# First K and V tiles of a linear attention kernel loaded as two transfers of 16 and 112 partitions

## The chip, the cores and the metric

One core of a Trainium2 chip runs the kernel. The metric is device time in microseconds (us). Before the change it is 126.86 us, the median of 3 runs (126.85 to 126.97).

## The reference

Linear attention with ReLU features, for 8 batches of 12 heads, 512 positions and 64 dimensions, in float32:

```python
Q_feat, K_feat = np.maximum(0, Q), np.maximum(0, K)
KV = np.einsum('bhkd,bhkv->bhdv', K_feat, V)          # 64 x 64 for each head
K_sum = np.sum(K_feat, axis=2)
numerator = np.einsum('bhqd,bhdv->bhqv', Q_feat, KV)
denominator = np.einsum('bhqd,bhd->bhq', Q_feat, K_sum)
return numerator / (denominator[..., None] + 1e-10)
```

Q, K, V and the output have 12.58 MB each, so 37.75 MB are read and 12.58 MB written.

## The kernel before

The 96 heads are worked in 12 octets of eight heads. An octet of K, V, Q or output is 1 MB of float32 that lies in one piece in memory; it is viewed as 128 partitions of 8 KB (`RQ * D` = 32 x 64 numbers), each partition being 32 positions of one head, so that 16 partitions make a head.

**Loads.** Octets 1 to 11 come through GpSimd's queue: `load_kv(g)` fetches K and V of four heads at a time (L99, L101), `load_q(o)` a whole Q octet (L105), all cast to bf16 on the way. They are issued in order in a loop at the top (L115 to L118); `kin` and `vin` have 12 buffers and `qin` 7. The K and V of octet 0 are the exception: they are loaded as float32, each by one transfer of 128 partitions, K from SyncE (SP, L111) and V from ScalarE (ACT, L112), into `k8` and `v8` (named `k_first` and `v_first` in the profile), two buffers of the pool that later holds the output tiles. The order of work is written out by hand; the tile framework adds only the waits that data needs.

**Octet 0.** `prep8` makes the bf16 operands: DVE writes `kf` (ReLU of K times a mask, L152) and half of `vo8` (V times a mask, L157), ACT the other half (L156). `qt(0)` transposes Q on TensorE (L208) and ACT applies the ReLU (L216). `mm_kv8` accumulates K^T V in PSUM over 32 matmuls (L163), and ACT copies the blocks out (L167).

**Octets 1 to 11.** `prep` and `prep_v` (L173, L175, L180, L182) make the operands of four heads, `mm_kv` (L187) the products, `evac_kv` (L197) the copies, `denom` (L258 to L270) the reciprocals of the denominators, `out_t` (L238, L240) the transposed numerators, `back` (L276) their transposes, and `norm` (L282) the product of the two on DVE.

**Stores.** `store(o)` issues one store of 1 MB from SP (L298), the last octet in two halves (L296). Ahead of each of the first seven stores SP issues a small transfer ("probe", L291) that reads 2 to 14 partitions of the K tile of five octets later, which holds the stores back until that tile has landed:

```python
    def store(o, o_sb):
        if o + DELAY < NO:
            n = PROBE[o]
            nc.sync.dma_start(out=scratch[0:n], in_=k_sb[2 * (o + DELAY)][0:n, 0, :])
```

Of the kernel before, what the change touches and what calls it, by code (L numbers as in the profile page):

```python
# [10 lines left out]
def kernel(  # L11
# [7 lines left out]
    nc = tc.nc  # L19
    B, H, S, D = Q.shape  # L20
    assert D == 64
    P = 128
# [35 lines left out]
    def view(X, f):  # L58
        return X.rearrange("b h s d -> (b h s d)").rearrange("(n p f) -> n p f", p=P, f=f)
# [43 lines left out]
    def load_q(o):  # L103
        q_sb[o] = qin.tile([P, U, 2 * D], bf16, name="q_sb")
        nc.gpsimd.dma_start(out=q_sb[o].rearrange("p u f -> p (u f)"), in_=Qr[o], single_packet=True)  # L105


    K8, V8 = view(K, RQ * D), view(V, RQ * D)
    k8 = outp.tile([P, RQ, D], fp32, name="k_first", tag="o_sb")
    v8 = outp.tile([P, RQ, D], fp32, name="v_first", tag="o_sb")  # L110
    nc.sync.dma_start(out=k8.rearrange("p r d -> p (r d)"), in_=K8[0])  # L111
    nc.scalar.dma_start(out=v8.rearrange("p r d -> p (r d)"), in_=V8[0])  # L112
    load_q(0)
    make_identity(nc, ident)
    for o in range(1, NO):  # L115
# [288 lines left out]
```

## Time and profile before

| | |
|---|---|
| median of 3 runs | 126.86 us |
| the profiled execution | 126.98 us |
| its span, first to last instruction | 125.2 us |
| busy share of the span: PE, DVE, ACT, POOL | 68%, 67%, 64%, 26% |
| HBM read and written over the span | 402 GB/s |
| DMA packets | 10349 |
| `k_first` and `v_first` issued | 0.74 us |
| first use of `k_first` (DVE L152) and `v_first` (ACT, before L156) | 9.55 and 9.81 us |
| first probe issued by SP | 43.19 us |

The profile is of one execution. Its busy shares are those of the compute engines; the DMA rows give the mean share of 16 DMA engines and the bytes that they moved (counted where they are written, so a load with a cast to bf16 counts half of what it reads). q0 is the queue of GpSimd's transfers, q1 that of SP's, q10 that of ACT's. "To landing" is the time from a transfer's issue until all of it has arrived. A stretch's DMA share can come out slightly over 1, since neighbouring packets of an engine overlap.

### The profile page before, as it was taken

The numbers are of one execution on the slowest core, as the hardware profiler recorded it, in microseconds if no ns is written. First come the engines' busy times: TensorE is split into PE (matmuls) and PEld (weight loads), VectorE is DVE, ScalarE is ACT, GpSimd is POOL, SyncE is SP. The second block draws the span as 40 slices with busy tenths as digits, with TensorE's granted clock in tenths as the row PEclk, the third lists the DMA queues.
The fourth block names the chain that finished last, engine by engine and source line by source line (L and its number), as shares of the span: only waits on it lengthen the run. The fifth ranks groups of instructions, "written<-read, shape, count | busy, mean of one in ns | idle before, by whom it ended". The sixth has DMA issues, their size and how long they took to land.

```text
span 125.2 us, 2684 instructions
## 1 busy us (share of the span) xinstructions
PE 85.7 (68%) x1075; PEld 77.4 (62%) x1075; DVE 83.5 (67%) x192; ACT 80.7 (64%) x112; POOL 32.1 (26%) x62
## 2 busy tenths in 40 slices
PE   0005795598988899895498499399777587797500
PEld 0005465497878789783597398299576486696400
DVE  2719715979799797979348746935928918979600
ACT  0008959969898998989159468666839646837100
POOL 6902624414344241142133124033122000000000
PEclk9999999999999999999679769959999999999995
DMA  2999999999999999999999999999999999999992
GB/s 84 390 325 205 217 205 209 219 202 217 205 214 210 209 215 320 263 213 290 294 212 276 310 211 249 334 213 216 349 232 217 330 254 212 321 423 424 424 412 116
DMA packets 10349, 32.68 MB, mean 261 GB/s; under 512 B 1249, under 2 KB 1249, under 8 KB 8673
## 3 DMA queue, kind: packets, MB, share of 16 engines
q0 software_dynamic: 8064, 17.83, 74.4%
q1 hardware_dynamic: 2128, 13.64, 26.8%
q10 hardware_dynamic: 144, 1.05, 2.1%
q8 instruction: 8, 0.13, 0.4%
q14 instruction: 5, 0.03, 0.1%
HBM read 37.75 MB, written 12.58 MB: 402 GB/s over the span
## 4 chain that ended last, share of the span: by engine, by line
DMA 33%; DVE 28%; PE 24%; ACT 5%; issue 3%; DVEq 1%; ACTq 0%; POOLq 0%
DMA v_sb<-in_V_dram 14%; DVE o_sb L282 13%; DMA q_sb<-in_Q_dram 13%; PE ps_kv L187 8%; DMA v_first<-in_V_dram 7%; PE ps_bk L276 6%; DVE kf L173 4%; PE ps_kv L163 4%; PE ps_qt L208 4%; DVE vo_all L175 3%; DVE vo_all L182 2%; ACT vo_all L156 2%; DVE den L266 2%; ACT qt L216 2%; DVE rec L270 1%
## 5 line engine op out<-in xcount | busy, mean ns | idle before, releaser
L282 DVE TENSOR_TENSOR o_sb<-ps_bk,rec 128x1024 f32<-128x1024 f32 x24 | 28.3, 1218 | 15.3 <-PE ps_bk L276 15.3
L187 PE MATMUL ps_kv<-vo_all,kf 128*128 128x132 bf16 x352 | 25.9, 232 | 6.6 <-DVE vo_all L182 6.1
L187 PEld LDWEIGHTS <-kf 128*128 128x128 bf16 x352 | 23.7, 104 | 7.9 <-issue 4.3
L208 PE MATMUL ps_qt<-ident,q_sb 128*128 128x128 bf16 x192 | 16.0, 250 | 16.7 <-DMA q_sb<-in_Q_dram 16.7
L216 ACT ACTIVATE qt<-ps_qt 128x1024 bf16<-128x1024 bf16 x23 | 22.4, 1024 | 6.3 <-PE ps_qt L208 6.2
L197 ACT CAST kvd<-ps_kv 64x260 bf16<-64x260 f32 (+1 forms) x46 | 16.6, 360 | 15.1 <-PE ps_kv L187 13.9
L208 PEld LDWEIGHTS <-q_sb 128*128 128x128 bf16 x192 | 14.2, 114 | 17.7 <-DMA q_sb<-in_Q_dram 17.6
L240 ACT COPY ot_sb<-ps_ot 128x1024 f32<-128x1024 f32 x22 | 22.0, 1014 | 1.9 <-PE ps_ot L238 1.0
L276 PE MATMUL ps_bk<-ident,ot_sb 128*128 128x128 f32 x192 | 23.0, 273 | 0.0
L173 DVE TENSOR_SCALAR kf<-k_sb,mask 128x1024 bf16<-128x1024 bf16 x44 | 18.3, 458 | 6.4 <-DMA k_sb<-in_K_dram 6.4
L99 POOL DMA_DIRECT2D k_sb<-in_K_dram x22 | 12.2, 555 | 37.1 <-DMA q_sb<-in_Q_dram 17.2
L276 PEld LDWEIGHTS ps_bk<-ident,ot_sb 128*128 128x128 f32 x192 | 20.8, 141 | 0.0
L101 POOL DMA_DIRECT2D v_sb<-in_V_dram x22 | 12.5, 566 | 18.3 <-DMA k_sb<-in_K_dram 10.2
L238 PE MATMUL ps_ot<-qt,kvd 128*128 128x256 bf16 x88 | 12.7, 271 | 4.3 <-DVE o_sb L282 4.3
L238 PEld LDWEIGHTS <-kvd 128*128 128x128 bf16 x88 | 8.2, 97 | 6.3 <-issue 5.7
L180 ACT ACTIVATE vo_all<-v_sb,mask 128x1024 bf16<-128x1024 bf16 x10 | 11.5, 1153 | 0.2
L175 DVE TENSOR_SCALAR vo_all<-v_sb,mask 128x1024 bf16<-128x1024 bf16 x22 | 10.7, 485 | 1.3 <-DMA v_sb<-in_V_dram 1.3
L258 PEld LDWEIGHTS <-qt 128*128 128x128 bf16 x192 | 6.7, 96 | 4.9 <-ACT qt L216 2.0
L258 PE MATMUL ps_den<-kvd,qt 128*128 128x16 bf16 x192 | 7.3, 179 | 3.0 <-ACT kvd L167 1.7
L105 POOL DMA_DIRECT2D q_sb<-in_Q_dram x12 | 7.0, 580 | 7.6 <-DMA v_sb<-in_V_dram 4.8
L156 ACT ACT_TABLE_LOAD x1 | 1.3, 1283 | 9.8 <-DMA v_first<-in_V_dram 9.8
L182 DVE TENSOR_SCALAR vo_all<-v_sb,mask 128x1024 bf16<-128x1024 bf16 x12 | 5.8, 484 | 0.0
(35 smaller groups left out, 48.3 us busy)
## 6 DMA issues: line engine op xcount, KB each, us to landing
out_dram<-o_sb SPq DMA_DIRECT2D x11, 1024.0 KB, 8.8
q_sb<-in_Q_dram POOLq DMA_DIRECT2D x12, 512.0 KB, 14.7
k_sb<-in_K_dram POOLq DMA_DIRECT2D x22, 256.0 KB, 14.1
v_sb<-in_V_dram POOLq DMA_DIRECT2D x22, 256.0 KB, 13.2
v_first<-in_V_dram ACTq DMA_DIRECT2D x1, 1024.0 KB, 9.0
k_first<-in_K_dram SPq DMA_DIRECT2D x1, 1024.0 KB
out_dram<-o_sb SPq DMA_DIRECT2D x2, 512.0 KB, 5.0
scratch<-k_sb SPq DMA_DIRECT2D x1, 1.0 KB
```

The costliest lines, as they stand in the source:

```text
L101: nc.gpsimd.dma_start(out=v_sb[g].rearrange("p r d -> p (r d)"), in_=Vr[g], single_packet=True)
L173: nc.vector.tensor_scalar(kf[g][:, :, s, :], k_sb[g], scalar1=0.0, scalar2=mask[:, 0, s:s + 1], op0=Alu.max, op1=Alu.mult)
L175: nc.vector.tensor_scalar(vo[g % NB][:, :, 0, 2:D + 2], v_sb[g], scalar1=mask[:, 1, 0:1], scalar2=None, op0=Alu.mult)
L187: nc.tensor.matmul(ps_kv[:, g % 2, 0:2 * (D + 2)].rearrange("p (t d) -> p t d", t=2), kf[g][:, r, :, :].rearrange("p s d -> p (s d)"), vo[ ...
L197: copy(kvd[o % NK][64 * c:64 * c + 64, 4 * gs.start + s:4 * gs.stop:2, c * D1:c * D1 + D1].rearrange("p (g t) d -> p g t d", t=2), ps_kv[6 ...
L208: nc.tensor.transpose(ps[:, u, :], q_sb[o][:, i * (U // 2) + u, :], ident)
L216: nc.scalar.activation(to, ps, Act.Relu)
L238: nc.tensor.matmul(ps[:, i], kvd[o % NK][:, h, 1:2 * D + 1], q[:, :, h, :], start=True, stop=True, skip_group_check=True)
L240: nc.scalar.copy(ot[o][:, :, 4 * j:4 * j + 4], ps.rearrange("p h u c -> p u h c"))
L258: nc.tensor.matmul(ps[:, u], qt_sb[o % NZ][:, u, :], kvd[o % NK][:, :, 0:2 * D1:2 * D1 - 1], start=True, stop=True, skip_group_check=True)
L276: nc.tensor.transpose(ps[:, 2 * v:2 * v + 2].rearrange("p c d -> p (c d)"), ot[o][:, 8 * j + v].rearrange("p h c -> p (h c)"), ident32)
L282: nc.vector.tensor_tensor(o_sb[:, rs], ps, rec[o][:, rs].unsqueeze(2).to_broadcast([P, 16, D]), op=Alu.mult)
```

## The change

The two loads of 128 partitions become four: partitions 0 to 15 of K (SP) and of V (ACT), and then partitions 16 to 127 of each, on the same two queues. The tiles, the bytes and all that follows are the same.

```diff
     k8 = outp.tile([P, RQ, D], fp32, name="k_first", tag="o_sb")
     v8 = outp.tile([P, RQ, D], fp32, name="v_first", tag="o_sb")
-    nc.sync.dma_start(out=k8.rearrange("p r d -> p (r d)"), in_=K8[0])
-    nc.scalar.dma_start(out=v8.rearrange("p r d -> p (r d)"), in_=V8[0])
+
+    for rows in (slice(0, 16), slice(16, P)):
+        nc.sync.dma_start(out=k8[rows].rearrange("p r d -> p (r d)"), in_=K8[0][rows])
+        nc.scalar.dma_start(out=v8[rows].rearrange("p r d -> p (r d)"), in_=V8[0][rows])
     load_q(0)
     make_identity(nc, ident)
```

## The prediction

> **What bounds the kernel now.** I read the page first (slices, queues, issues), then the busy time by stretch at both ends, then the chain of waits and the timeline of the first microseconds. The slices and the queues:
>
> ```profile
> span 125.2 us, 2684 instructions
> ...
> DMA  2999999999999999999999999999999999999992
> GB/s 84 390 325 205 217 205 209 219 202 217 205 214 210 209 215 320 263 213 290 294 212 276 310 211 249 334 213 216 349 232 217 330 254 212 321 423 424 424 412 116
> ...
> q1 hardware_dynamic: 2128, 13.64, 26.8%
> q10 hardware_dynamic: 144, 1.05, 2.1%
> ```
>
> From the second slice to the last but one the 16 DMA engines are at 9 of 10, while no compute engine passes 68% of the span. (The rates near 210 are loads that GpSimd issues with a cast to bf16, so the bytes written are half of those read; the engines are as full there.) Only the first slice (0 to 3.1 us) and the last have room. The two ends in the view of busy time by stretch (columns: stretch, its length, PE, PEld, DVE, ACT and POOL busy, clock, DMA share, GB/s):
>
> ```profile
> 1.50:2.00 0.50, 0.00 (x0) 0.00 (x0) 0.25 (x1) 0.00 (x0) 0.50 (x2) 1.00 0.40 66
> 2.00:2.50 0.50, 0.00 (x0) 0.00 (x0) 0.17 (x3) 0.00 (x0) 0.42 (x3) 1.00 0.46 131
> 2.50:3.00 0.50, 0.00 (x0) 0.00 (x0) 0.23 (x3) 0.00 (x0) 0.50 (x2) 1.00 0.85 262
> 3.00:3.50 0.50, 0.00 (x0) 0.00 (x0) 0.23 (x3) 0.00 (x0) 0.50 (x1) 1.00 0.81 344
> 3.50:4.00 0.50, 0.00 (x0) 0.00 (x0) 0.17 (x2) 0.00 (x0) 0.50 (x2) 1.00 1.02 426
> ...
> 115.00:120.00 5.00, 2.60 (x26) 2.30 (x23) 3.08 (x4) 1.16 (x2) 0.00 (x0) 1.00 1.00 422
> ```
>
> The engines take two microseconds to get from nothing to 426 GB/s, and only `k_first` and `v_first` feed them then. At 115 to 120 us they run at 422 GB/s on stores alone. Is that the end of a queue, or the pace of compute? The timeline and the issues answer:
>
> ```profile
> 0.74 0.41 ACTq L112 DMA_DIRECT2D v_first<-in_V_dram  x1
> 0.74 0.39 SPq L111 DMA_DIRECT2D k_first<-in_K_dram  x1
> 1.24 0.66 POOL L105 DMA_DIRECT2D q_sb<-in_Q_dram  x1 [0.79 <-POOLq L388]
> ```
>
> ```profile
> v_first<-in_V_dram ACTq DMA_DIRECT2D x1, 1024.0 KB, 9.0
> ...
> out_dram<-o_sb SPq DMA_DIRECT2D x2, 512.0 KB, 5.0
> ```
>
> A last half store moves 524 KB, 1.24 us at 422 GB/s, yet takes 5.0 us to land: about 3.8 us of stores stand before it. So compute has some 3.8 us to spare at the tail, and the kernel ends when the DMA engines have moved everything. The chain of waits agrees in the middle: it runs through compute until 47.5 us, then sits on `v_sb` landing (14% of the span) and `q_sb` landing (13%). A microsecond of DMA time lost or won at the start therefore reaches the end whole.
>
> **Part 1: issues and packets, priced at nothing on the path.** One more issue on SP (0.39 us, by the L111 row) and one on ACT (0.41 us, L112). SP's next instruction is the first probe at 43.2 us; ACT's is the table load before L156, which waits for V until 9.81 us. If that cover were gone they would cost 0.4 us each. GpSimd's Q load at 1.24 us is on a sequencer of its own and is not moved. The second K transfer is queued behind the first on SP and issues at about 1.13 to 1.52 us; the present one issued at 0.74 and its first bytes move after 1.5 us, so it should be there by some 2.3 us. Packets: in q10, 144 are 128 rows of 8 KB and 16 completions. In q1, 128 rows of K, 11 x 128 and 2 x 128 rows of stores, and the seven probes' 56 rows make 1848; 14 whole transfers give 224 completions, which leaves 56, one for each row of the probes. So a transfer of few rows goes one row to an engine, and one of 16 rows puts one 8 KB row on each of the 16. A row at full rate is 8192 B by 426/16 GB/s = 0.31 us. The 32 added completions are 2 small packets per engine, a few hundredths of a microsecond at most.
>
> **Part 2: the ramp, a gain.** Summing the stretches, by 4.0 us (0.5 x (66+131+262+344+426)) KB = 615 KB have moved, which is 1.44 us at 426 GB/s: the ramp is worth a start at 4.0 - 1.44 = 2.56 us. The first bytes move in the stretch from 1.5 us; if rows on all engines began at about 1.8, that would be 0.75 us better. If the ramp is the time in which a transfer's rows are handed out, a transfer of an eighth of the rows shortens it; if it is the latency of the first reads, it stays. Bounds 0 and -0.75, and nothing in the trace separates them; I take -0.3, nearer to nothing because the share of 0.40 to 0.46 with little moved says that engines already hold packets and wait on them.
>
> **Part 3: the 16-row slices, a loss.** K's rows 0 to 15 and V's rows 0 to 15 (262 KB) now stand at the head of both hardware queues on every engine, and the other rows are behind them. At 426 GB/s they take 0.62 us, as the same bytes do now. [...] Bounds: 0.62 us (nothing lost) and, at the 66 GB/s of the poorest stretch, 4.0 us (3.4 lost). I take the 131 GB/s of 2.0 to 2.5 us, the stretch nearest to this case: both queues under way, but not all engines delivering. 262 KB by 131 GB/s is 2.0 us, so +1.4. The rows behind do not fill the hole, since they are behind on the same queues, and Q's load has not arrived (GpSimd's transfers move only when the GB/s fall below 400, after 5 us).
>
> [...]
>
> **Part 4: the other 112 rows.** [...] Bounds: at 426 GB/s the remaining 1.84 MB take 4.3 us, nothing lost; at 344 GB/s, the poorest stretch with both queues full, 5.3 us, so +1.0. I take +0.4, below the middle since GpSimd's loads join from 5 us and fill what is left free.
>
> **Part 5: waits.** DVE's L152 and ACT's L156 wait for two completions instead of one. Behind L152 stands all of DVE, behind L156 the copies that PE's L163 needs. A wait by itself is 17 ns (the semaphore instructions at L298). K and V would land 1 to 2 us later than now (9.6 and 9.7 us), and the compute chain starts later by as much; that hides under the loads it waits for from 47.5 us on and the 3.8 us at the tail, and the loads themselves are late by the same amount.
>
> **Sum:** -0.3 + 1.4 + 0.4 + 0.0 = +1.5 us. The profiled execution took 126.98 us (span 125.2 and 1.8 around it), so 128.5 by it; the median of the runs is 0.12 lower, and so I forecast 128.4 us.
>
> **Rivals.**
>
> *The early start pays (faster).* The 16 rows go through at 426 GB/s and wake all engines at once; the second transfers arrive before the two rows per engine (0.62 us) are done. Price: part 2 at its -0.75 end or less, parts 3 and 4 at nothing: 126.1 to 126.5 us, middle 126.3. For it: the ramp is the only unfilled stretch before the tail, and every engine gets a row. It decides where the two slices take less than about 1.0 us together, since then part 3 costs less than the ramp gives. [...] Chance 0.28.
>
> *It moves nothing (same).* Either the slices' loss and the ramp's gain cancel (0.4 to 0.7 us each), or the ramp is read latency and the 16 rows flow freely, which leaves the completions: 126.7 to 127.0 us. For it: the same bytes move by the same engines. Chance 0.08.
>
> *The bad end of my own case.* The slices at 66 GB/s and the 112 rows at +1.0 would give +3.4 + 1.0 - 0.3 = +4.1, 131.0 us. Both ends together are unlikely; I count 0.07 for anything above 129.8, inside the chance of slower.
>
> **How the numbers follow.** Slower 0.64 (forecast, 127.2 to 129.8 its own range), same 0.08, faster 0.28; "same" is within 0.2%, 0.25 us, about what a measurement of this kernel can tell from no change. The range: 129.8 leaves 0.07 above; reaching down to 126.2 takes in most of the rival, with about 0.08 below. That is 126.2 to 129.8.
>
> **What would show it.** Right or wrong on part 1: q10 with 160 packets and q1 with 2144. Part 3: a stretch of about 2 us after 1.8 us with a high DMA share at 100 to 150 GB/s; the rival would show 400 GB/s before 3 us. Part 4: 340 to 426 GB/s afterwards, `v_first` landing past 10.5 us. The end: the first probe on SP, now at 43.2 us, and the last stores later by the same 1.5 us; stores at 422 GB/s to the last. I am wrong if K and V land before 9.5 us, or if they land late and the probes do not move.

## The result and the profile after

The change makes the kernel slower: 129.05 us (median of 4 runs, 128.95 to 129.19) against 126.91 us, a ratio of 1.0169 with a 95% interval of 1.0152 to 1.0187. The profiled execution took 129.19 us, its span is 127.4 us against 125.2.

The slices and queues of the changed kernel's page:

```profile
span 127.4 us, 2689 instructions
...
DMA  5999999999999999999999999999999999999993
GB/s 95 221 293 233 211 217 205 210 212 208 214 208 221 202 214 269 309 215 241 334 216 239 342 215 216 345 234 219 305 271 214 301 279 214 304 413 419 427 405 148
...
q1 hardware_dynamic: 2144, 13.64, 27.7%
q10 hardware_dynamic: 160, 1.05, 3.1%
```

The two queues have the 16 more packets each that 16 more completions make. The DMA engines are as full as before, and even fuller in the first slice (5 tenths against 2), but the second and third slices move 221 and 293 GB/s where they moved 390 and 325. From the fourth on the two rows look alike. So the engines are busy and deliver less, at the start only. Packets overlap a little: over the whole span the queues' shares add up to 104.4% of the 16 engines' time (103.8% before the change). The stretches of the start say when (columns as before: stretch, length, the five engines, clock, DMA share, GB/s). They count a packet, with all its time and its bytes, in the stretch in which it starts; that is how a share can be 1.57, well over 1:

```profile
1.50:2.00 0.50, 0.00 (x0) 0.00 (x0) 0.25 (x1) 0.00 (x0) 0.50 (x2) 1.00 0.87 197
2.00:2.50 0.50, 0.00 (x0) 0.00 (x0) 0.17 (x3) 0.00 (x0) 0.42 (x3) 1.00 1.40 246
2.50:3.00 0.50, 0.00 (x0) 0.00 (x0) 0.23 (x3) 0.00 (x0) 0.50 (x2) 1.00 0.77 98
3.00:3.50 0.50, 0.00 (x0) 0.00 (x0) 0.23 (x3) 0.00 (x0) 0.50 (x2) 1.00 1.57 164
3.50:4.00 0.50, 0.00 (x0) 0.00 (x0) 0.17 (x2) 0.00 (x0) 0.50 (x2) 1.00 0.66 82
4.00:5.00 1.00, 0.00 (x0) 0.00 (x0) 0.92 (x5) 0.00 (x0) 1.00 (x3) 1.00 0.83 213
5.00:6.00 1.00, 0.00 (x0) 0.00 (x0) 0.89 (x3) 0.00 (x0) 1.00 (x3) 1.00 1.01 295
6.00:8.00 2.00, 0.00 (x0) 0.00 (x0) 0.53 (x13) 0.00 (x0) 0.16 (x1) 1.00 0.97 281
```

Three phases can be read from it. To 2.5 us the changed kernel is ahead by the rows that have started: 0.5 x (197+246) = 222 KB against 98 KB, a lead of 123 KB or 0.29 us at 426 GB/s. From 2.5 to 5 us it moves 98, 164, 82 and 213 GB/s where the kernel before moved 262, 344, 426 and 410; by 5.0 us it has 607 KB against 1025, 0.98 us behind. From 5 to 8 us it runs at 281 to 295 GB/s, and there it loses the rest. The queues from 5 to 7 us (packets, MB, share of the 16 engines' time), before the change and then after it:

```profile
q1 hardware_dynamic: 37, 0.30, 37.1%
q10 hardware_dynamic: 37, 0.30, 36.0%
q0 software_dynamic: 31, 0.13, 31.4%
```

```profile
q10 hardware_dynamic: 37, 0.30, 52.1%
q1 hardware_dynamic: 33, 0.27, 46.0%
```

The same 37 rows of V took 36.0% of the engines' 2 us and now take 52.1%: 0.31 and 0.45 us a row (share x 2 us x 16 engines / 37). GpSimd's loads (q0) have no packet here after the change; their first ones come in the stretch from 7 to 8 us, two microseconds later than before. The loads behind them are late as well: the first probe on SP, whose time is set by a load of octet 5, is issued at 45.25 us, 2.06 later.

```profile
45.25 0.78 SPq L293 DMA_DIRECT2D scratch<-k_sb  x1
```

After that nothing is lost or won; the span ends 2.2 us later. K and V are first used at 12.3 and 12.4 us, 2.7 and 2.6 us later than before:

```profile
12.26 1.42 DVE L154 TENSOR_SCALAR kf<-k_first,mask8k 128x1024 bf16<-128x1024 f32 x2 [5.45 <-DMA k_first<-in_K_dram]
12.43 1.28 ACT L158 ACT_TABLE_LOAD   x1 [12.43 <-DMA v_first<-in_V_dram]
```

### The profile page after: what moved, and what is told of

The parts are those of the page before. It is cut to its first block, busy times and chain, and to the rows that moved or that the text cites. A ratio compares the mean times of both kernels' runs of the same rounds, so it can differ in the third digit from the quotient of the medians.

```text
span 127.4 us, 2689 instructions
## 1 busy us (share of the span) xinstructions
PE 88.0 (69%) x1075; PEld 78.8 (62%) x1075; DVE 83.4 (65%) x192; ACT 80.6 (63%) x112; POOL 31.4 (25%) x62
## 3 DMA queue, kind: packets, MB, share of 16 engines
q1 hardware_dynamic: 2144, 13.64, 27.7%
## 4 chain that ended last, share of the span: by engine, by line
DMA 77%; PE 8%; DVE 6%; issue 2%; POOL 2%; DVEq 1%; ACT 0%; POOLq 0%
DMA k_sb<-in_K_dram 31%; DMA q_sb<-in_Q_dram 25%; DMA v_sb<-in_V_dram 21%; DVE o_sb L284 4%; PE ps_bk L278 4%; PE ps_kv L189 2%; DVEq L401 1%; PE ps_qt L210 1%; DVE kf L175 1%; DVE qt L216 1%; PE ps_den L227 1%; POOL q_sb L105 0%; PE ps_ot L253 0%; DVE kvd L199 0%; ACT kvd L199 0%
## 5 line engine op out<-in xcount | busy, mean ns | idle before, releaser
L210 PE MATMUL ps_qt<-ident,q_sb 128*128 128x128 bf16 x192 | 15.2, 243 | 19.1 <-DMA q_sb<-in_Q_dram 19.1
L210 PEld LDWEIGHTS <-q_sb 128*128 128x128 bf16 x192 | 13.5, 110 | 20.3 <-DMA q_sb<-in_Q_dram 20.1
L278 PE MATMUL ps_bk<-ident,ot_sb 128*128 128x128 f32 x192 | 24.0, 280 | 0.0
L278 PEld LDWEIGHTS ps_bk<-ident,ot_sb 128*128 128x128 f32 x192 | 21.9, 146 | 0.0
L240 PE MATMUL ps_ot<-qt,kvd 128*128 128x256 bf16 x88 | 13.6, 284 | 4.4 <-DVE o_sb L284 4.4
L101 POOL DMA_DIRECT2D v_sb<-in_V_dram x22 | 11.9, 542 | 18.2 <-DMA k_sb<-in_K_dram 11.7
L177 DVE TENSOR_SCALAR vo_all<-v_sb,mask 128x1024 bf16<-128x1024 bf16 x22 | 10.6, 483 | 1.2 <-DMA v_sb<-in_V_dram 1.2
L158 ACT ACT_TABLE_LOAD x1 | 1.3, 1283 | 12.4 <-DMA v_first<-in_V_dram 12.4
L165 PE MATMUL ps_kv<-vo_all,kf 128*128 128x264 bf16 x32 | 6.1, 379 | 1.0 <-ACT vo_all L158 1.0
```

What stands on the lines that cost most here:

```text
L101: nc.gpsimd.dma_start(out=v_sb[g].rearrange("p r d -> p (r d)"), in_=Vr[g], single_packet=True)
L210: nc.tensor.transpose(ps[:, u, :], q_sb[o][:, i * (U // 2) + u, :], ident)
L240: nc.tensor.matmul(ps[:, i], kvd[o % NK][:, h, 1:2 * D + 1], q[:, :, h, :], start=True, stop=True, skip_group_check=True)
L278: nc.tensor.transpose(ps[:, 2 * v:2 * v + 2].rearrange("p c d -> p (c d)"), ot[o][:, 8 * j + v].rearrange("p h c -> p (h c)"), ident32)
```

## The experiments

Three theories were set against each other. **Destination**: a transfer is slow where the rows that the 16 engines move at one time land in neighbouring partitions. **Start**: the second transfer on a queue pays a start of its own, wherever its rows go. **Source**: 16 engines read one small piece of memory at once. All differences below are to the median of the kernel before on the same chip (126.91, 127.02 and 126.97 us in the three sets). The edits replace the two loads of `k8` and `v8`; `kf8` and `vf8` are their flat views; the listings leave out lines that are the same, and where one stands for several kernels a comment says how they differ. In all of them DVE and ACT wait for all of K and V.

### The two transfers in the other order

```diff
-    for rows in (slice(0, 16), slice(16, P)):
+    for rows in (slice(0, 112), slice(112, P)):
```

> The same two transfers in the other order: partitions 0 to 111 first, then the 16 partitions 112 to 127. Destination theory (a transfer is slow where the rows that the engines move at one time land in neighbouring partitions, 16 rows worst, 112 rows less): the start ramps as before the change, then K and V flow at the 280 to 310 GB/s that the changed kernel showed between 5 and 10 us, and the 16-row slices come last; about +1.3 to +2.2 us against before. Start theory (the second transfer on a queue pays a start of its own, the 1.2 us that the first rows of the 112 took at 3 to 4 us): the second start now falls while Q and the next loads flow, so 0 to +0.5 us, and 420 GB/s from 3.5 us on.

Measured: 131.30 us, +4.39, ratio 1.0336 (1.0314 to 1.0358). Worse than either theory said. The 112 rows by themselves are slow from the moment the ramp ends, in the stretches:

```profile
4.00:5.00 1.00, 0.00 (x0) 0.00 (x0) 0.94 (x5) 0.00 (x0) 1.00 (x3) 1.00 1.03 262
5.00:6.00 1.00, 0.00 (x0) 0.00 (x0) 0.89 (x3) 0.00 (x0) 1.00 (x3) 1.00 0.97 262
```

That is 262 GB/s at full engines. The queues of these 2 us have nothing but 64 rows of 8 KB, with no completion of a transfer among them and no load of GpSimd's:

```profile
q1 hardware_dynamic: 32, 0.26, 51.1%
q10 hardware_dynamic: 32, 0.26, 49.0%
```

A row takes 0.51 and 0.49 us, with no slice ahead and no second transfer yet moving, so the start theory cannot account for it. The slices, now last, move beside GpSimd's loads at 133 and 145 GB/s (10 to 14 us), where the kernel before moved 204 to 210 on those loads alone: a slice in the middle of other traffic holds that up too, which I had not priced.

### Cut by columns instead of partitions

```diff
+    for cols in (slice(0, 256), slice(256, RQ * D)):
+        nc.sync.dma_start(out=kf8[:, cols], in_=K8[0][:, cols])
+        nc.scalar.dma_start(out=vf8[:, cols], in_=V8[0][:, cols])
```

> The same bytes in a first and a second transfer (one eighth, seven eighths), but cut by columns: all 128 partitions take part in both, 1 KB and then 7 KB of each row. Destination theory: no loss, -0.6 to +0.3 us against before. Start theory: the second start stays where it was, after an eighth of the bytes: +1 to +2 us.

Measured: 128.12 us, +1.21, ratio 1.0088 (1.0064 to 1.0113). By the number this is the start theory's. The stretches tell more:

```profile
2.50:3.00 0.50, 0.00 (x0) 0.00 (x0) 0.23 (x3) 0.00 (x0) 0.50 (x2) 1.00 0.70 113
3.00:3.50 0.50, 0.00 (x0) 0.00 (x0) 0.23 (x3) 0.00 (x0) 0.50 (x1) 1.00 0.66 57
3.50:4.00 0.50, 0.00 (x0) 0.00 (x0) 0.17 (x2) 0.00 (x0) 0.50 (x2) 1.00 0.72 113
...
5.00:6.00 1.00, 0.00 (x0) 0.00 (x0) 0.89 (x3) 0.00 (x0) 1.00 (x3) 1.00 1.05 425
```

From 5 us on it flows at 425 GB/s, so the second loss of the changed kernel is absent where all 128 partitions take part. The first is there, but the run has a fault as a test: its first transfers are 256 rows of 1 KB, and those go at 57 to 156 GB/s between 2 and 3.5 us, with the engines not even full (0.62 to 0.70). It measures small rows as much as a second start. It left the start theory standing for the time to 5 us.

### Eight slices of 16 partitions, and V turned

```diff
+    for i in range(8):
+        rows = slice(16 * i, 16 * i + 16)
+        to = rows        # the second kernel: V goes 64 partitions further, modulo 128
+        nc.sync.dma_start(out=kf8[rows], in_=K8[0][rows])
+        nc.scalar.dma_start(out=vf8[to], in_=V8[0][rows])
```

> All of the first K and V in eight transfers of 16 partitions each, K and V in the same order. Destination theory: 2.1 MB at the 82 to 164 GB/s of the changed kernel's stretches from 2.5 to 4 us (mean 115) would take 18 us in place of 5, less where the engines fall out of step: +6 to +13 us. Start theory: seven more starts of 1 to 2 us: +7 to +14 us. This run alone does not tell them apart; it is the base for the next.

> The eight transfers of 16 partitions again, the same sources in the same order, but each V slice is put 64 partitions further on (V's halves change places, so this kernel multiplies K with the wrong rows of V; nothing else differs in work). Destination theory: K and V no longer crowd the same partitions, so the loss of the eight slices falls to half or less of the run with both in the same order: +2 to +5 us. Start theory, and any theory of the reading side: the same time as with both in the same order, within 0.5 us. [...]

Measured: 138.27 us, +11.36, ratio 1.0901 (1.0869 to 1.0932) with both in the same order; 136.01 us, +9.10, ratio 1.068 (1.0622 to 1.0737) with V turned. The second is a miss for the destination theory as I had worked it out. It is a miss for "the same within 0.5 us" as well, but nearer to it. My working had a gap: if the engines take a row of K and a row of V in turn, and all in step, then at any one time only one slice is being written, and where V goes does not matter. The queues of the turned run, from 1.5 to 2.2 us and from 2.2 to 2.8 us, do begin so, 16 rows of K and then 16 of V:

```profile
q1 hardware_dynamic: 16, 0.13, 75.5%
```

```profile
q10 hardware_dynamic: 16, 0.13, 123.7%
```

The repair was made after the fact, so the theory needed a test of its own.

### Destination and source taken apart

Four times eight transfers of 16 rows on each queue; only which rows they read and which partitions they fill differ.

```diff
+    for i in range(8):
+        near, apart = slice(16 * i, 16 * i + 16), slice(i, P, 8)
+        src, dst = apart, apart      # the others: (apart, near) and (near, apart)
+        nc.sync.dma_start(out=kf8[dst], in_=K8[0][src])
+        nc.scalar.dma_start(out=vf8[dst], in_=V8[0][src])
```

> Eight transfers of 16 rows each on both queues, as in the run with eight slices (11.3 us slower than before), but transfer i takes the partitions i, i+8, ..., i+120, in the source and in the tile. Start theory (each further transfer on a queue costs about 10 us / 7 = 1.4 us, whatever its rows): the same +11 us. Destination theory, now with the engines in step (all 16 are on a row of K at one time and on a row of V the next, which is why moving V alone to other partitions won back only 1 to 2 us): the loss falls to half or less, +2 to +5 us. Source theory (16 engines reading one 128 KB piece of memory at a time): also +0 to +5. [...]

> The eight transfers again, sources 8 rows apart, destinations 16 neighbouring partitions (K and V are permuted alike, so the heads are mixed up; nothing else differs in work). Destination theory: as slow as the eight slices were, +10 to +12 us. Source theory: as fast as the run with both apart. Start theory: +11 us.

> The eight transfers again, sources 16 neighbouring rows (one piece of 128 KB), destinations 8 partitions apart (heads are mixed up here too). Destination theory: as fast as the run with both apart, +2 to +5 us. Source theory: as slow as the eight slices, +10 to +12 us. Start theory: +11 us.

| | source near | source 8 apart |
|---|---|---|
| destination near | +11.36 us (the eight slices) | +9.93 us, ratio 1.0778 (1.0715 to 1.0842) |
| destination 8 apart | +2.21 us, ratio 1.0177 (1.0149 to 1.0204) | +2.47 us, ratio 1.0197 (1.0181 to 1.0212) |

The destination decides: moving it apart is worth 7.5 to 9.2 us, moving the source apart 1.4 us at most. Same bytes, same number of transfers, same row size. The start theory, which wanted +11 in all four, falls; so does the source theory. What makes up the 2.2 to 2.5 us of the lower row is not divided. The queues of K (q1) and V (q10) from 1 to 24 us, 128 rows and 128 completions each, first with near destinations and sources apart, then the reverse:

```profile
q10 hardware_dynamic: 256, 1.05, 39.8%
q1 hardware_dynamic: 256, 1.05, 32.6%
```

```profile
q1 hardware_dynamic: 256, 1.05, 17.0%
q10 hardware_dynamic: 256, 1.05, 16.7%
```

The same rows hold the engines for 72.4% and for 33.7% of these 23 us, about 1.0 and 0.5 us a row. Their V is first used at 23.07 and at 16.99 us.

Into the near slices 2.1 MB went in some 22 us (1.8 to 24.1 us in the run with K and V in the same order), 94 GB/s with other loads beside them. The runs show that the time depends on the destination; what in the chip makes it so was not measured.

### Steps of seven

Seven transfers of 16 partitions that lie 7 apart, and then the last 16 partitions:

```diff
+    for i in range(8):
+        rows = slice(i, 112, 7) if i < 7 else slice(112, P)
```

> [...] Destination theory: the seven lose what the 112 rows lost in the run with 112 first by 10 us (1.5 to 2 us), and the last slice as much as there (1.5): +2 to +4 us. Start theory: +11 us. [...]

Measured: 129.45 us, +2.43, ratio 1.021 (1.0159 to 1.0261). In the range, and no +11. It does not divide the loss between the seven and the last slice, whose price beside other loads was shown by the first experiment to be large (133 and 145 GB/s); on the 112 rows it says little, since no run shows that the engines take 112 rows in such steps.

### The first slices by themselves

```diff
+    for q, x in ((nc.sync, K8), (nc.scalar, V8)):
+        spare = outp.tile([P, RQ * D], fp32, name="spare", tag="o_sb")
+        q.dma_start(out=spare[0:16], in_=x[0][0:16])      # the other kernel: spare[0:P:8]
+    nc.sync.dma_start(out=kf8, in_=K8[0])
+    nc.scalar.dma_start(out=vf8, in_=V8[0])
```

> Measures the first slices by themselves: rows 0 to 15 of K and of V are loaded twice, first into 16 neighbouring partitions of spare tiles that nobody reads, and then with the whole tiles, each as one transfer of 128 partitions as before the change. 262 KB more, 0.62 us at 426 GB/s. Destination theory: 0.62 plus the 1.0 to 1.1 us that the changed kernel had fallen behind by 5 us, so +1.6 to +1.8 us. If the changed kernel's whole loss came from its 112 rows, only +0.4 to +0.7.

> The same extra load of 16 rows, put into partitions 8 apart. Destination theory: the 0.62 us of its bytes and little else, +0.4 to +1.0 us. A cost of the second transfer on a queue, wherever the first one goes: as much as with neighbouring partitions.

Measured: 128.17 us, +1.20, ratio 1.0102 (1.0086 to 1.0117) into neighbouring partitions; 127.77 us, +0.80, ratio 1.0063 (1.0049 to 1.0077) into partitions 8 apart. Less 0.62 us for the added bytes (an estimate: 262 KB at 426 GB/s) that is 0.58 and 0.18. The first lies between the two expectations: the slices cost something, not the whole 1.0. The second says that a second transfer behind a short one costs little in the end, 0.18 us (0.0 to 0.4 by the interval), though GpSimd's loads help there: they already take 52.6% of the engines' time from 3 to 4 us. So the +1.21 of the cut by columns is more than a second start accounts for. The stretches of the run with neighbouring partitions:

```profile
2.50:3.00 0.50, 0.00 (x0) 0.00 (x0) 0.23 (x3) 0.00 (x0) 0.50 (x2) 1.00 0.97 98
3.00:3.50 0.50, 0.00 (x0) 0.00 (x0) 0.23 (x3) 0.00 (x0) 0.50 (x2) 1.00 1.43 164
3.50:4.00 0.50, 0.00 (x0) 0.00 (x0) 0.17 (x2) 0.00 (x0) 0.50 (x2) 1.00 0.18 33
4.00:5.00 1.00, 0.00 (x0) 0.00 (x0) 0.92 (x5) 0.00 (x0) 1.00 (x3) 1.00 0.86 295
5.00:6.00 1.00, 0.00 (x0) 0.00 (x0) 0.89 (x3) 0.00 (x0) 1.00 (x3) 1.00 1.02 426
```

The same hole as in the changed kernel to 4 us (98, 164, then little), and then 426 GB/s. The slices' 262 KB have all started by 2.5 us here, so the hole is the first rows of what stands behind them. Those that start from 3 to 4 us take about 1.0 us each; behind the slices 8 apart they take 0.5. After it the two runs part: behind the same slices, whole transfers of 128 partitions recover at once, while the 112 rows go on at 281 to 295. So the two losses are separate, and the second belongs to the 112 rows.

### K alone

```diff
+    for rows in (slice(0, 16), slice(16, P)):
+        nc.sync.dma_start(out=kf8[rows], in_=K8[0][rows])
+    nc.scalar.dma_start(out=vf8, in_=V8[0])
```

> Only K is split into 16 and 112 partitions, V stays one transfer. Destination theory: half of the loss of the change or a little more, since V's well-spread rows also wait on engines that are held up by K's: +1.0 to +1.6 us. Start theory: the whole, +2.1 us, if one late queue is enough, otherwise half.

Measured: 126.89 us, -0.08, ratio 1.0001 (0.9992 to 1.001): no difference, where both theories wanted at least 1 us. The stretches and the first uses of the two tiles:

```profile
2.00:2.50 0.50, 0.00 (x0) 0.00 (x0) 0.17 (x3) 0.00 (x0) 0.42 (x3) 1.00 0.87 164
2.50:3.00 0.50, 0.00 (x0) 0.00 (x0) 0.23 (x3) 0.00 (x0) 0.50 (x2) 1.00 0.56 115
3.00:3.50 0.50, 0.00 (x0) 0.00 (x0) 0.23 (x3) 0.00 (x0) 0.50 (x1) 1.00 0.92 279
3.50:4.00 0.50, 0.00 (x0) 0.00 (x0) 0.17 (x2) 0.00 (x0) 0.50 (x2) 1.00 1.03 426
4.00:5.00 1.00, 0.00 (x0) 0.00 (x0) 0.92 (x5) 0.00 (x0) 1.00 (x3) 1.00 1.04 434
```

```profile
6.75 1.28 ACT L158 ACT_TABLE_LOAD   x1 [6.75 <-DMA v_first<-in_V_dram]
...
10.78 1.42 DVE L154 TENSOR_SCALAR kf<-k_first,mask8k 128x1024 bf16<-128x1024 f32 x2 [3.97 <-DMA k_first<-in_K_dram]
```

One 16-row slice leaves a short hole (115 GB/s from 2.5 to 3.0 us), which the early start pays for. Then V runs alone at 426 to 434 GB/s and is there by 6.75 us, and K comes after it, by 10.78. The queues from 4 to 5 us and from 6 to 9 us:

```profile
q10 hardware_dynamic: 53, 0.43, 104.3%
```

```profile
q1 hardware_dynamic: 80, 0.66, 54.4%
q0 software_dynamic: 73, 0.30, 49.0%
```

In this run K's 112 rows and V's rows hardly share the engines, and K's rows, with GpSimd's loads beside them, take 0.33 us each: they cost nothing that shows. So the loss is not half per tensor. 112 rows of one tensor run at nearly full pace beside other loads (0.33 us a row, against 0.31 at 426 GB/s), and 112 rows of both at once do not (0.45 to 0.51 us). Whether they would be slow beside a whole transfer of 128 was not tested, since the two did not meet here. Why the two sets of 112 rows slow each other is open too: that they meet on destinations is argued from the 16-row slices, and no run shows which partitions an engine fills when 112 rows are cut. So is why K's second transfer waited for V.

### A try for a faster version

```diff
+    wake = consts.tile([16, 2, 16], fp32, name="wake")
+    nc.sync.dma_start(out=wake[:, 0], in_=K8[0][0:16, 0:16])
+    nc.scalar.dma_start(out=wake[:, 1], in_=V8[0][0:16, 0:16])
+    nc.sync.dma_start(out=kf8, in_=K8[0])
+    nc.scalar.dma_start(out=vf8, in_=V8[0])
```

> A try for a faster version: both tiles in one transfer each, as before the change, with a transfer of 16 partitions of 64 bytes ahead on each queue that nobody reads. If the ramp is the engines' first read, this takes it off: -0.1 to -0.4 us. If it is the time in which 128 rows are handed out, the second issue comes 0.4 us later on both queues and is all that is left: +0.2 to +0.5 us.

Measured: 127.08 us, +0.11, ratio 1.0014 (1.0005 to 1.0023). It does not pay, and it lies between the two expected ranges, in neither:

```profile
2.00:2.50 0.50, 0.00 (x0) 0.00 (x0) 0.17 (x3) 0.00 (x0) 0.42 (x3) 1.00 2.20 263
2.50:3.00 0.50, 0.00 (x0) 0.00 (x0) 0.23 (x3) 0.00 (x0) 0.50 (x2) 1.00 0.00 0
```

The first 16 rows of K's whole transfer start between 2.0 and 2.5 us and take 1.1 us each (2.20 x 0.5 us x 16 engines / 16), so they fill the next half microsecond, in which no packet starts. These rows have no slice ahead of them: slow first rows are not the slices' alone, and what makes these slow is open. 344 GB/s is reached in the stretch from 3.5 us, where the kernel before reached it from 3.0. No version tried beats the kernel before; splitting K alone equals it.

## Why the prediction was right

The direction, the bound and the sum held: +1.5 us forecast, +2.14 measured, inside the range. By its steps:

- **What bounds the kernel: right.** 2.06 us late at the first probe, 2.2 us longer in the span, 2.14 in the median. The DMA time lost at the start went to the end nearly whole, and no compute engine passes 69% of the span after the change (PE).
- **Part 1, issues and packets: right.** 2144 and 160 packets; no issue shows on the path. The small packets that make up the completions took about 0.02 us each before the change (9 to 10 us: six in q10, 0.8% of the 16 engines' time). One transfer ahead of another costs about 0.2 us (0.18, the extra load into partitions 8 apart).
- **Part 2, the ramp: right in size.** A lead of 0.29 us by 2.5 us, against -0.3. That it fits so well is luck: the -0.3 was picked between 0 and -0.75 with no row to pick it by. A short first transfer gets more rows going early (222 KB by 2.5 us against 98); a wake-up of small rows did not keep that gain (+0.11 us).
- **Part 3, the slices: a loss as forecast, the size too high.** No run shows the +1.4: that neighbouring partitions make a transfer slow was my assumption, with no row of 8 KB into them in the trace before, and the 131 GB/s came from a row of the ramp, which has no slice in it. What the runs showed in its place: with the same extra load, destinations apart in place of neighbouring ones saved 0.40 us (+0.80 against +1.20). That the mean from 2 to 4 us came to 148, near the 131, is in part luck. The 32 rows of the slices all start between 1.5 and 2.95 us, at 181 GB/s in the mean, and take about 0.7 us each in place of 0.31; the 164 and 82 GB/s from 3 to 4 us are no longer theirs but the first rows of K's 112 behind them, at about 1.1 us each. Slices and ramp together were put at +1.4 - 0.3 = +1.1; the extra load into neighbouring partitions measures them at 0.58, and the stretches of the changed kernel, which has its first 112 rows in them, at 0.98 by 5 us.
- **Part 4, the 112 rows: the step that failed in size.** I took +0.4 and bounded it at +1.0; that rows cut at other places meet on destinations was my assumption, and no run shows it for the 112 rows. What is left of 2.14 is 1.56 us after the 0.58, and still 1.16 after the 0.98: beyond my bound by either count. Its bound was the 344 GB/s of a stretch of the ramp; the 112 rows ran at 262 to 295, a row in 0.45 to 0.51 us in place of 0.31. I had also expected GpSimd's loads from 5 us on to fill what was free. They came from 7 us on, and there was nothing free: the engines were busy on slow rows. The sign said 340 to 426 GB/s afterwards, and 281 to 295 came.
- **Part 5, waits: right in kind.** K and V came 2.6 to 2.7 us later, more than the 1 to 2 forecast, and the end moved by no more than the loads did (2.06 us at the first probe).

Two errors of opposite sign, -0.5 in parts 2 and 3 and +1.2 in part 4 (-0.1 and +0.8 by the count of the stretches), made the sum better than its terms; to that extent the forecast was lucky. The faster rival's condition, the two slices done in less than about 1.0 us, did not come: the first of their rows start before 2.0 us and the last after 2.5, and a row takes about 0.7 us. With only one slice, in the run with K alone split, the early start and the hole did cancel, as the second rival had it for the two.

## What to carry to other kernels

Where the DMA engines are the bound, read a change of a transfer's shape by where its rows land at one time, not by its bytes: the same 2.1 MB in the same number of transfers cost 2.2 us or 11 us more, by the destination alone. Cut a load by partitions only with a reason, since the piece that looks whole (112 of 128) can lose more than the small one (here 1.56 us against 0.58, or 1.16 against 0.98). When a term has no row in the trace, do not bound it by rows of well-behaved transfers; and test each half of a symmetric change by itself, since two streams at once may cost what one of them alone does not (here +2.14 us against -0.08).

## What the runs showed of the hardware that I had not expected

- Busy is not moving: a DMA share of 0.97 to 1.09 stood beside 131 GB/s (the eight slices in the same order, 4 to 5 us), 262 and 426 GB/s of the same 8 KB float32 rows.
- Splitting one of two loads cost nothing (ratio 1.0001) where splitting both cost 2.14 us.
- In the run with K alone split, the second transfer on SP's queue hardly shared the engines with the whole transfer on ACT's: its tile was first used 4.0 us after V's (10.78 and 6.75 us), although it was issued by 1.6 us.
- With eight transfers to a queue, SP's issues stretched over 10.0 to 13.6 us, where one transfer of 128 partitions took 0.39 us to issue. What held them up is not shown.
- Rows of 1 KB at the start went at 57 to 156 GB/s between 2 and 3.5 us.
- GpSimd's first load, issued at 1.24 us before and after the change, had its first packets only between 5 and 6 us and between 7 and 8 us, with K's and V's rows on the engines until then; behind slices 8 partitions apart, GpSimd's loads had 52.6% of the engines' time from 3 to 4 us.
